# High weight tiles first, alternating lead products, and new address pads in the MLPs of a two-layer trunk

## The chip, the cores and the metric

The kernel runs on one core of one Trainium2 chip. The metric is the device time of one execution in microseconds (us); less is better. The profile is one execution on the same kind of core, taken by the hardware profiler.

## The reference

Two layers on a residual stream of 512 tokens by 1024 features, float32. The first layer mixes with multi-head latent attention, the second with gated linear attention; each is followed by an MLP with a squared ReLU. The change concerns the two MLPs (and the norm ahead of each), which hold most of the arithmetic.

```python
D_MODEL = 1024; SEQ = 512; D_FF = 4 * D_MODEL

def sq_relu_mlp(xn, w_up, w_down):
    hid = jnp.square(jax.nn.relu(xn @ w_up))
    return hid @ w_down

for i in range(DEPTH):                      # DEPTH = 2
    xn = rms_norm(x, norm_mix[i])
    mix = mla_mixer(xn, ...) if i == 0 else gla_mixer(xn, ...)
    x = x + mix.astype(x.dtype)
    x = x + sq_relu_mlp(rms_norm(x, norm_mlp[i]), mlp_w_up[i], mlp_w_down[i])
return rms_norm(x, final_norm)
```

## The kernel before

**Float32 products from three matmuls.** TensorE (PE) works on a rounded float32 type. Each operand is therefore split into a high tile (the value rounded, made by a copy on ScalarE, ACT) and a low tile (the rest, made by a subtraction on VectorE, DVE); this is `split` (L105 to L113, ACT at L110, DVE at L113). A product takes three matmuls: high weight times high input (L118), high weight times low input (L119), low weight times high input (L120), in `mm3`. `piece` makes the high and low tiles of a weight, `wh` and `wl`, in three rotating buffers each. One split of 128 by 1024 elements is shared by the 24 matmuls of a product, each with a weight of 128 by 128 and a moving operand of 128 by 256.

**Seven products in place of eight.** The MLP's two matrix products are computed block by block with the Winograd form of Strassen's scheme. `up_block(b)` makes 512 of the 4096 hidden features, in two halves of 256; the inner dimension of 1024 is split in a leading and a trailing half, the tokens in a first and a second half. Its seven products have the names "11", "21", "22" (plain inputs x0 to x3, x4 to x7) and "T1" to "T4" (combinations of inputs, tiles T0 to T3 by feature pair, made by `QuadNorm.pair`). The weights are loaded by `unit`, the combined weights are made on DVE (L884, L899, L905, L912). The steps are s0 to s7; s0 only loads and splits the first two weights of block 0, s1 is product "11", s2 "21", s5 "T1", s6 "T2", s3 "22", s7 "T3", s4 "T4". Steps end in `finish`, which multiplies by the norm's factor `rstd` (DVE, L840) and squares (ACT, L841).

`down_block(s)` takes two up blocks back to the residual stream, again in seven products (p1 to p7) of two pieces each, with the hidden values as moving operand: tile `h`, split by `operand`. The last two up blocks go through `down` or `down_final` with ordinary products. Sums stay in the tiles `sum1`, `sum6`, `sum7` and in the residual stream's own tiles `xT`.

**The lead of an MLP.** `out_proj` ends the mixer in four steps c = 0 to 3. Each adds two column tiles to `xT`, scales them for the norm (`scaled`), squares them (`square`), and makes one of the four pairs (`pair(c)`). At c = 3 it starts the MLP (`next(after)`): only s0 runs. When the projection is done the MLP goes on: the pools `stage` and `ps` close, `down` and `down_w` open, and the lead runs the steps of `lead = [blocks[b].pop(0) for b in (0, 0, 1, 1)]`: block 0's s1, then `begin` (the norm's mean by a matmul with a constant tile, L253, then `rstd`, and four subtractions in the residual stream, L1080), block 0's s2, block 1's s1, block 1's s2. Block 1's first weights (both halves of the inner dimension) come in one load of 1024 KB into the pool `down_w` (L824). After the lead the remaining steps run block by block with `down_block` steps between them.

**Order of work.** The program names the work in the order of the source; the order in each engine's queue is then chosen by a scheduler, which may move an instruction ahead of others when it takes it to be ready sooner. `tc.keep_in_program_order(i)` holds an instruction behind everything that the source has named on its engine so far; `with tc.issue_after(i)` holds what the block names on i's engine behind i. Neither makes an engine wait for an instruction's end.

**Addresses.** Pools take addresses from the left or the right end of on-chip memory, and `pad` puts some bytes (`PADS`) into a pool so that the tiles behind it move. All weight and operand tiles are multiples of 512 bytes long, so one number, the distance of the moving operand from the weight tile modulo 512 bytes, holds for all matmuls of a group. `right` and `up` move the up operands, `stage` the pools on the left.

## Time and profile before

| what | value |
|---|---|
| median of 3 runs | 1093.47 us (1093.22 to 1094.63) |
| the profiled execution, its own time | 1092.46 us |
| span of its instructions | 1090.7 us |
| PE busy in the span | 1065.7 us (98%), 7322 matmuls |
| weight loads | 981.1 us (90%) |
| DVE busy | 892.1 us (82%) |
| ACT busy | 641.0 us (59%) |
| HBM traffic | 99 GB/s over the span |

PE is the matrix engine, PEld its weight loads, DVE and ACT the two elementwise engines, POOL the general one, SP the engine whose queue issues most loads. A row of a timeline has the start in us from the span's start, the duration, engine, line, operation, tile written and tiles read, shape and count; in brackets the idle time of the engine before it and what ended it. A row of busy time by window has the stretch, its length, and for each engine the busy time and the number of instructions, then the granted clock of PE (1.00 is full), the busy share of the DMA engines and their GB/s. Ends of matmuls are modelled: the distance between two starts is what a matmul really took.

### The profile page before, as it was taken

To read this page: it belongs to the slowest core of one execution; us is meant where nothing else is said; L and a number is where in the kernel's file an instruction comes from. 1 tells how busy PE (TensorE), PEld (TensorE's weight loads), DVE (VectorE), ACT (ScalarE), POOL (GpSimd) and SP (SyncE) were. 2 spreads that over 40 slices of the span, in tenths; PEclk is the share of its full clock that TensorE was granted. 3 is DMA by queue.
4 is the path that set the end of the run, shared out by engine and by line. 5 is a ranking of instruction groups with operands and counts; after the bars stand their busy time and mean duration, and the time that the engine had idled before them with its cause. 6 is when DMAs were issued, how large, how long until landed. Compare 5 with 4: busy or idle time off the path is not lost.

```text
span 1090.7 us, 17825 instructions
## 1 busy us (share of the span) xinstructions
PE 1065.7 (98%) x7322; PEld 981.1 (90%) x7322; DVE 892.1 (82%) x1210; ACT 641.0 (59%) x934; POOL 46.6 (4%) x78
## 2 busy tenths in 40 slices
PE   8999999899999999999999999999999999999997
PEld 6788888889999999998788888887999999999986
DVE  6789878899899899977565655678899899799865
ACT  6577655555667677654334735655565666766734
POOL 6400000000000000030000000000000000000000
PEclk9999999999999999999999999999999999999999
DMA  7312113633433422251222222125424424522312
GB/s 215 87 49 78 29 32 92 198 97 117 149 104 98 155 97 97 78 190 42 53 73 78 78 78 63 53 78 173 132 65 132 141 78 133 167 71 94 134 41 78
DMA packets 99057, 108.93 MB, mean 100 GB/s; under 512 B 8112, under 2 KB 73920, under 8 KB 98976
## 3 DMA queue, kind: packets, MB, share of 16 engines
q1 hardware_dynamic: 96960, 106.57, 31.0%
q10 hardware_dynamic: 1952, 1.21, 0.4%
q8 instruction: 57, 0.93, 0.4%
q0 software_dynamic: 64, 0.02, 0.1%
q14 instruction: 24, 0.20, 0.1%
HBM read 105.69 MB, written 2.10 MB: 99 GB/s over the span
## 4 chain that ended last, share of the span: by engine, by line
PE 87%; DVE 8%; ACT 2%; issue 1%; DMA 1%; SPq 0%; ACTq 0%; DVEq 0%
PE ps L118 27%; PE ps L120 27%; PE ps L119 26%; DVE wl L113 2%; PE ps L135 2%; PE ps L1345 2%; ACT wh L110 1%; DMA wraw_ckv<-in_mla_w_in_dram 1%; DVE raw L1000 1%; DVE raw L884 1%; DVE h L113 0%; PE ps L1382 0%; PE ps L666 0%; DVE raw L912 0%; PE ps L667 0%
## 5 line engine op out<-in xcount | busy, mean ns | idle before, releaser
L110 ACT ACTIVATE wh<-raw 128x1024 fp32r<-128x1024 f32 x210 | 221.3, 1057 | 177.4 <-PE ps L119 135.9
L113 DVE TENSOR_TENSOR wl<-raw,wh 128x1024 fp32r<-128x1024 f32 x210 | 254.4, 1218 | 25.4 <-ACT wh L110 24.9
L120 PE MATMUL ps<-h,wl 128*128 128x256 f32 x672 | 188.4, 280 | 2.6 <-DVE wl L113 2.5
L118 PE MATMUL ps<-h,wh 128*128 128x256 f32 x672 | 187.9, 280 | 0.0
L119 PE MATMUL ps<-h,wh 128*128 128x256 f32 x672 | 187.8, 280 | 0.0
L120 PEld LDWEIGHTS ps<-h,wl 128*128 128x128 f32 x672 | 126.5, 188 | 3.8 <-DVE wl L113 3.8
L118 PEld LDWEIGHTS ps<-h,wh 128*128 128x128 f32 x672 | 126.3, 188 | 0.0
L119 PEld LDWEIGHTS ps<-h,wh 128*128 128x128 f32 x672 | 126.3, 188 | 0.0
L118 PE MATMUL ps<-set,wh 128*128 128x512 f32 x232 | 91.4, 395 | 1.3 <-ACT set L243 1.3
L119 PE MATMUL ps<-set,wh 128*128 128x512 f32 x232 | 90.8, 391 | 1.0 <-DVE set L244 1.0
L120 PE MATMUL ps<-set,wl 128*128 128x512 f32 x232 | 90.6, 390 | 0.0
L110 ACT ACTIVATE wh<-wraw 128x1024 fp32r<-128x1024 f32 x41 | 43.0, 1056 | 73.9 <-PE ps L120 41.5
L118 PE MATMUL ps<-wh,set 128*128 128x512 f32 x144 | 59.7, 414 | 0.0
L841 ACT ACTIVATE q<-q 128x512 f32<-128x512 f32 x64 | 40.1, 627 | 32.0 <-DVE q L840 31.9
L113 DVE TENSOR_TENSOR wl<-wraw,wh 128x1024 fp32r<-128x1024 f32 x41 | 50.0, 1222 | 10.6 <-ACT wh L110 10.5
L113 DVE TENSOR_TENSOR h<-q,h 128x1024 fp32r<-128x1024 f32 x42 | 51.2, 1218 | 7.5 <-ACT h L110 7.5
L120 PE MATMUL ps<-wh,set 128*128 128x512 f32 x144 | 56.4, 391 | 0.0
L119 PE MATMUL ps<-wl,set 128*128 128x512 f32 x144 | 56.2, 391 | 0.0
L119 PEld LDWEIGHTS ps<-set,wh 128*128 128x128 f32 x232 | 43.6, 188 | 11.0 <-DVE set L244 2.2
L118 PEld LDWEIGHTS ps<-set,wh 128*128 128x128 f32 x232 | 43.5, 188 | 11.0 <-ACT set L243 2.0
L120 PEld LDWEIGHTS ps<-set,wl 128*128 128x128 f32 x232 | 43.6, 188 | 8.9
L110 ACT ACTIVATE h<-q 128x1024 fp32r<-128x1024 f32 x42 | 44.1, 1050 | 1.3 <-DVE q L986 1.3
(490 smaller groups left out, 3003.9 us busy)
## 6 DMA issues: line engine op xcount, KB each, us to landing
raw<-in_mlp_w_down_dram SPq DMA_DIRECT2D x38, 1024.0 KB, 5.2
raw<-in_mlp_w_up_dram SPq DMA_DIRECT2D x62, 512.0 KB, 3.8
wraw<-in_gla_w_in_dram SPq DMA_DIRECT2D x11, 1024.0 KB, 5.2
wraw<-in_mla_w_o_dram SPq DMA_DIRECT2D x8, 512.0 KB, 4.8
wraw<-in_gla_w_o_dram SPq DMA_DIRECT2D x8, 512.0 KB, 4.9
raw<-in_mlp_w_up_dram SPq DMA_DIRECT2D x2, 1024.0 KB, 7.7
xT<-in_x_dram SPq DMA_DIRECT2D x6, 256.0 KB, 7.6
wraw_qn<-in_mla_w_uq_dram SPq DMA_DIRECT2D x6, 256.0 KB, 3.4
```

Of the source, the lines that this page charges most:

```text
L110: order(ACT.activation(hi, src, AF.Copy))
L113: lo_eng.tensor_tensor(lo, src, f(hi), ALU.subtract)
L118: PE.matmul(psum, wh, xh, start=start, stop=False, **kw)
L119: PE.matmul(psum, wh, xl, start=False, stop=False, **kw)
L120: PE.matmul(psum, wl, xh, start=False, stop=stop, **kw)
L135: PE.transpose(psum, src, ident[: src.shape[0], : src.shape[0]])
L841: ACT.activation(qs, qs, AF.Square)
L884: DVE.tensor_tensor(s, v["a21"], v["a22"], ALU.add)
L1000: DVE.tensor_tensor(v["S"], v["12"], v["S"], ALU.subtract)
L1345: PE.matmul(p[:, t * 64 : (t + 1) * 64].rearrange("p (n c) -> p n c", c=m), k[:, sl], later, start=True, stop=True)
```

## The change

Five things are done. In the diff, `raised` collects the ACT copies that `split` issues and `cut_at` the DVE subtractions of `piece`; `made` holds the tiles that a block finds made already.

- Inside `matmuls`, which up and down products share, all matmuls with high weight tiles are issued first, for each weight with the high and the low input, and then all with low weight tiles. An up product's two output halves are now both inside one call. The first matmul of each call is held behind everything that the source has named on PE before it.
- The lead runs block 0's s1, block 1's s1, the mean's matmul, then block 0's s2 and block 1's s2. Block 1's first weights come in two loads of 512 KB (`ahead`), with the block's other up loads queued behind them, and its high and low tiles are made ahead of block 0's s1.
- The fourth pair is no longer made in `out_proj` but in the lead, in two parts, `combine` (into a buffer of tag `q` of the pool `down`) and `combined` (its split); `combine` is queued behind the low tile of block 1's "11", the low tile of block 1's "21" behind the combination, the pair's split behind that.
- The four subtractions in the residual stream move behind block 0's last split.
- Pads: `hidden` puts 416 bytes ahead of `h` in the first MLP's `down` pool; `up` goes from 448 to 320 bytes in the second MLP; `down_w` gets 224 bytes in the second MLP.

```diff
-    PADS = dict(stage=224, right=64, up=448, masks=256, keep=128)
+    PADS = dict(stage=224, right=64, up=(448, 320), masks=256, keep=128, hidden=(416, 0), down_w=(0, 224))
...
+    raised, cut_at = [], []
...
+        def mean(self):
+            self.ms = bank("c")
+            return PE.matmul(self.ms, self.inv, self.acc, start=True, stop=True)
...
         def pair(self, k):
             pool = pool_of("up")
+            self.combined(k, self.combine(k, pool.tile([P, 4, TH], F32, tag="raw", bufs=5, name=uname("raw"))))
+
+        def combine(self, k, t):
...
+            return t
+
+        def combined(self, k, t):
...
+            i = split(t, hi, lo)
...
+            return i
...
-            nxt.pair(c)
+            if c < 3:
+                nxt.pair(c)
...
         def matmuls(p, w, k0, ks, ms, x, begin, end):
-            for k in ks:
-                for m in ms:
-                    mm3(
-                        p[:, m * TH : (m + 1) * TH],
-                        cut(w, slice(None), k - k0, slice(m * P, (m + 1) * P)),
-                        x[k],
-                        begin and k == 0 and m % 2 == 0,
-                        end and k == 3,
-                        skip_group_check=True,
-                    )
+            def one(i, j, k, m, start, stop):
...
+            steps = [(k, m) for k in ks for m in ms]
+            for k, m in steps:
+                i = one(0, 0, k, m, begin and k == 0 and m % 2 == 0, False)
+                if (k, m) == steps[0]:
+                    tc.keep_in_program_order(i)
+                one(0, 1, k, m, False, False)
+            for k, m in steps:
+                one(1, 0, k, m, False, end and k == 3)
...
             def unit(half, trail):
                 if b == 1 and half == 0:
-                    if not trail:
-                        c0 = b * FB
-                        t = wide_raw().rearrange("p a (b n) -> p (a b) n", b=2)
-                        SP.dma_start(t, w_up[:, c0 : c0 + 256].rearrange("(k p) n -> p k n", p=P))
-                        v["a12"] = t[:, KH:]
-                    return t[:, :KH]
+                    return ahead[trail]
                 t = up.tile([P, KH, 256], F32, tag="raw", bufs=5, name=uname("raw"))
                 c0 = b * FB + half * 256
-                SP.dma_start(t, w_up[trail * 512 : trail * 512 + 512, c0 : c0 + 256].rearrange("(k p) n -> p k n", p=P))
+                with tc.issue_after(made["load"].ins) if "load" in made else nullcontext():
+                    SP.dma_start(t, w_up[trail * 512 : trail * 512 + 512, c0 : c0 + 256].rearrange("(k p) n -> p k n", p=P))
                 return t
 
             def product(p, a, name, begin):
                 w = v.pop(name) if name in v else piece(a, KH, 256)
-                for j in range(2):
-                    matmuls(p, w, 0, range(KH), [j], quad[name], begin, True)
+                matmuls(p, w, 0, range(KH), range(2), quad[name], begin, True)
...
         def down_block(s):
             last = s == NB // 2 - 2
+            if s == 0:
+                pad(dp, PADS["hidden"][layer])
...
-        def begin():
-            nrm.finish()
-            for k in range(KH):
-                DVE.tensor_tensor(xT[k][:, second], xT[k][:, second], xT[k + KH][:, second], ALU.subtract)
...
-        opened("down_w")
+        pad(opened("down_w"), PADS["down_w"][layer])
...
-        lead = [blocks[b].pop(0) for b in (0, 0, 1, 1)]
-        for i, step in enumerate(lead):
-            step()
-            if i == 0:
-                begin()
+        t = wide_raw().rearrange("p a (b n) -> p (a b) n", b=2)
+        ahead = t[:, :KH], t[:, KH:]
+        for i, a in enumerate(ahead):
+            made["load"] = SP.dma_start(a, w_up[i * 512 : i * 512 + 512, FB : FB + 256].rearrange("(k p) n -> p k n", p=P))
+        kept = tc.keep_in_program_order
+        made[1]["11"] = piece(ahead[0], KH, 256)
+        with tc.issue_after(raised[-1].ins):
+            blocks[0].pop(0)()
+        blocks[1].pop(0)()
+        with tc.issue_after(cut_at[-1].ins):
+            t = nrm.combine(KH - 1, dp.tile([P, 4, TH], F32, tag="q", bufs=6, name=uname("q")))
+        kept(nrm.mean())
+        made[1]["21"] = piece(ahead[1], KH, 256)
+        kept(cut_at[-1])
+        kept(nrm.combined(KH - 1, t))
+        pad(up, PADS["up"][layer])
+        nrm.finish()
+        for b in range(2):
+            blocks[b].pop(0)()
         downs = []
         for b in range(NB):
...
+            if b == 0:
+                with tc.issue_after(cut_at[-1].ins):
+                    for k in range(KH):
+                        DVE.tensor_tensor(xT[k][:, second], xT[k][:, second], xT[k + KH][:, second], ALU.subtract)
```

## The prediction, made before the result was known

> **What bounds the kernel now.** I read the profile page first, then busy time by window over the two MLPs, then the timelines of PE, ACT, DVE and SP where PE waited.

> ```profile
> span 1090.7 us, 17825 instructions
> PE 1065.7 (98%) x7322; PEld 981.1 (90%) x7322; DVE 892.1 (82%) x1210; ACT 641.0 (59%) x934; POOL 46.6 (4%) x78
> PE 87%; DVE 8%; ACT 2%; issue 1%; DMA 1%; SPq 0%; ACTq 0%; DVEq 0%
> L110 ACT ACTIVATE wh<-raw 128x1024 fp32r<-128x1024 f32 x210 | 221.3, 1057 | 177.4 <-PE ps L119 135.9
> ```

> The chain that ended last is PE for 87% of the span, so a change gains where PE waits or where a matmul takes longer than it must. The 8% that is DVE lies mostly in the MLPs, which the change touches:

> ```profile
> core 0: us, PE busy (x) PEld busy (x) DVE busy (x) ACT busy (x) POOL busy (x), PEclk, DMA share, GB/s
> 191.20:475.70 284.50, 277.48 (x2356) 274.92 (x2355) 265.71 (x249) 184.48 (x213) 5.58 (x8) 0.99 0.38 121
> 750.20:1036.60 286.40, 278.78 (x2357) 275.96 (x2356) 265.65 (x248) 185.49 (x214) 0.00 (x0) 0.99 0.38 122
> ```

> The first window is the first MLP from its first product to its last quarter-product, the second the same of the second MLP. Of 284.5 us DVE is busy 265.7: a second engine is only 19 us behind PE, and no gain of PE can outrun it. Each window holds 1344 matmuls of up products (56 products of 24) and 1008 of down products.

> Now the lead, the first products of the first MLP, on PE:

> ```profile
> 193.95 0.28 PE L120 MATMUL ps<-x3h,wl 128*128 128x256 f32 x1
> 199.03 0.38 PE L118 MATMUL ps<-x0h,wh 128*128 128x256 f32 x1 [0.93 <-ACT wh L110]
> 199.25 0.28 PE L119 MATMUL ps<-x0l,wh 128*128 128x256 f32 x1
> 201.28 0.58 PE L120 MATMUL ps<-x0h,wl 128*128 128x256 f32 x1 [1.76 <-DVE wl L113]
> 201.66 0.42 PE L118 MATMUL ps<-x1h,wh 128*128 128x256 f32 x1
> 204.22 0.28 PE L118 MATMUL ps<-x1h,wh 128*128 128x256 f32 x1
> 206.19 0.38 PE L118 MATMUL ps<-x4h,wh 128*128 128x256 f32 x1 [0.51 <-ACT mt L867]
> 226.98 0.39 PE L118 MATMUL ps<-x4h,wh 128*128 128x256 f32 x1 [1.08 <-ACT mt L888]
> 758.02 0.39 PE L118 MATMUL ps<-x0h,wh 128*128 128x256 f32 x1 [0.93 <-ACT wh L110]
> 760.28 0.38 PE L120 MATMUL ps<-x0h,wl 128*128 128x256 f32 x1 [1.75 <-DVE wl L113]
> ```

> A matmul is drawn 0.28 us long but the next normally starts 0.11 to 0.12 later, and the one behind a stall again takes 0.1 too long, so a stall costs its bracket plus 0.28. The second block's first product waits 1.21 for its high weight tile, then, after two matmuls, 2.04 for the low one; the next start is 0.38 later instead of 0.12, 0.26 more than normal, of which 0.1 is counted. From 201.66 to 204.22 lie twelve starts, 0.213 us each: PE ran at half clock after these waits, 1.15 us lost. With 0.79 at 206.19 the lead's stalls cost 1.21 + 2.04 + 0.16 + 1.15 + 0.79 = 5.35 us. The second MLP repeats them (758.02, 760.28).

> **The lead (part one).** Before, the products run b0-11, b0-21, b1-11, b1-21 ("b0-11": first block, half 0, operand 11), and b1's weights are the late ones:

> ```profile
> 188.44 0.39 SPq L824 DMA_DIRECT2D raw<-in_mlp_w_up_dram  x1
> 197.93 2.93 ACT L110 ACTIVATE wh<-raw 128x1024 fp32r<-128x1024 f32 x3
> raw<-in_mlp_w_up_dram SPq DMA_DIRECT2D x2, 1024.0 KB, 7.7
> 201.75 1.22 DVE L113 TENSOR_TENSOR wl<-raw,wh 128x1024 fp32r<-128x1024 f32 x1
> ```

> Their load is issued at 188.44, lands 7.7 later at 196, is raised by ACT from 197.9 and cut by DVE up to about 202.9, after everything that DVE does for the norm, for x7 and for the fourth pair. After, two loads of half the size are queued ahead of the block's other loads. Their buffer no longer shares bytes with the stage pool: by the tile sizes, the first wide tile begins 224 bytes below the end of the stage pool's last tile; 416 bytes of pad in the first MLP and 224 in the second take it clear, so the load need not wait for that tile. The transfer moves from 191 to 206, where the DMA engines are 0.73 busy (row below), to before 191, where they are 0.23 (row of 176 to 191 under the rivals). SP then holds back only b0's two loads of half 1, which the T1 product needs some 12 us later. The high tile's buffer comes free with the last matmul of the output projection (190.8, b0-11 starting at 191.2), so ACT raises b1-11 by 192.1 and DVE, right after its addition at 191.2, cuts it by 193.3. PE runs b0-11 to 194.0, b1-11 to 196.7, the mean's matmul (0.95 as before, 193.95 to 194.90), b0-21 to 200.4, b1-21 to 203.1. DVE in the meantime has x7's low part and square (0.66, 0.6), the pair's four combinations (0.4 each), b1-21's cut and T3's (1.14 each start to start): 6.1 us from 193.3, done by 199.5, before b1-21 starts. Queued behind those cuts are the three steps of rstd and T1's sum and cut, some 5 us to 204.5, and with low tiles late in a product T1 can start at 203.1 on its high tile. The mean waits for acc only if the scheduler puts the combinations ahead of it, 1.6 us. So the 5.35 us go; what is late next is DVE:

> ```profile
> 191.00:206.00 15.00, 11.99 (x79) 10.77 (x77) 14.59 (x20) 8.02 (x11) 0.00 (x0) 0.89 0.73 250
> 206.00:221.00 15.00, 14.81 (x128) 14.65 (x129) 12.43 (x12) 7.48 (x10) 0.00 (x0) 1.00 0.48 141
> 221.00:236.00 15.00, 13.79 (x114) 13.19 (x113) 13.16 (x15) 9.96 (x13) 0.00 (x0) 1.00 0.45 142
> 236.00:244.00 8.00, 7.18 (x63) 7.18 (x64) 8.00 (x9) 4.59 (x7) 0.00 (x0) 1.00 0.00 0
> ```

> In 53 us DVE is busy 48.2, idle 4.8. Its work there stays: the four subtractions of L1080 (0.42 each) move from before the lead's end to behind the first block's last cut, which puts about 1.2 us more into this stretch, and T1's sum (1.2), whose raw weights can now land before 191, may move out into DVE's idle time there. So I count 4.8 per MLP, 9.6 in all, between 0 (DVE takes all back) and 10.8. The stall at 226.98 waits for an ACT copy and is left.

> **High tiles first (part two).** A product issued high, high, low per weight; now all 16 high matmuls, then the 8 low. No instruction is added, and a loss I exclude: each matmul keeps its operands, and down products switch between PSUM regions every three matmuls already. The low tile is wanted by the 17th matmul instead of the 3rd, 14 x 0.113 = 1.6 us later, and a high buffer is free after the 16th instead of the 23rd, 0.8 us sooner, for which ACT's L110 idles 135.9 us in all (page row above). The pin on each call's first matmul forbids PE to begin a product ahead of its turn, as it did before 206.19, where two matmuls of T1 stood ahead of b1-21; behind that pin waits all of PE. I cost it at nothing, since the products' weights are made in the same order on ACT and DVE; should one be late out of turn, PE waits as at 226.98, 1.3 us a time. The stalls on low tiles behind the leads:

> ```profile
> 356.60 0.38 PE L120 MATMUL ps<-T0h,wl 128*128 128x256 f32 x1 [0.81 <-DVE wl L113]
> 404.48 0.39 PE L120 MATMUL ps<-h,wl 128*128 128x256 f32 x1 [0.34 <-DVE wl L113]
> 450.42 0.39 PE L120 MATMUL ps<-h,wl 128*128 128x256 f32 x1 [0.62 <-DVE wl L113]
> 917.27 0.38 PE L120 MATMUL ps<-T0h,wl 128*128 128x256 f32 x1 [0.93 <-DVE wl L113]
> 1011.33 0.38 PE L120 MATMUL ps<-h,wl 128*128 128x256 f32 x1 [1.54 <-DVE wl L113]
> ```

> With 0.28 each they cost 1.09 + 0.62 + 0.90 + 1.21 + 1.82 = 5.64. All but a fraction of the last fit into 1.6 us. But DVE is late there because it is behind, and a PE that does not wait meets the next late tile sooner. I take two thirds, 3.8; the ends are 0 and 5.6.

> **The addresses (part three).** Pads cost no instruction. They move the moving operand against the weight tiles. From the allocation: weight tiles lie at 416 modulo 512 bytes, up operands at 480 (64 beyond), the down operand h at 192 (288 beyond). After, h in the first MLP and up operands in the second stand 192 beyond; the first MLP's up stays at 64, the second's down at 288. What the trace shows of distances:

> ```profile
> 244.86 0.28 PE L118 MATMUL ps<-h,wh 128*128 128x256 f32 x1
> 250.47 0.28 PE L118 MATMUL ps<-x4h,wh 128*128 128x256 f32 x1
> 255.92 0.28 PE L118 MATMUL ps<-h,wh 128*128 128x256 f32 x1
> 407.16 0.28 PE L118 MATMUL ps<-x4h,wh 128*128 128x256 f32 x1
> 412.82 0.28 PE L118 MATMUL ps<-h,wh 128*128 128x256 f32 x1
> 619.67 0.28 PE L118 MATMUL ps<-set,ADh 128*128 128x256 f32 x1
> 621.47 0.28 PE L118 MATMUL ps<-set,ADh 128*128 128x256 f32 x1
> ```

> Forty-eight down matmuls at 288 take 244.86 to 250.47, 117 ns each; forty-eight up at 64 take 113.5; the same at 407.16 takes 117.9; fifteen at distance 0 (619.67 to 621.47) 120. So 64 has two beats, kept from one stall to the next. In the second MLP it ran about half and half: the window's 286.4 less 12.5 of stalls, 0.8 of the mean and 1008 x 117, over 1344, is 115.6. Distance 192 is nowhere in the trace. Its ends are 113.3 and 120; 288 is nearest (96 bytes, 64 is 128 away), so I take 117.0: down unchanged, up 1344 x 1.4 = +1.9 us. By the ends: down -3.7 to +3.0, up -3.1 to +5.9.

> [...]

> **Sum.** -9.6 - 3.8 + 1.9 = -11.5 on the profiled execution's 1092.46 (span 1090.7), 1081.0. The median of the runs, 1093.47, is 1.0 above it: 1082.0.

> **Rivals.** (a) Distance 192 keeps the fast beat, 113.3 throughout: -13.4 - 6.8, 1073.3. For it: 64 does so for long stretches; against: nothing shows it for 192. (b) Addresses do nothing at 192, the beats following stalls alone: -13.4, 1080.1. [...] (c) DVE is the bound of the lead and gives all of part one back: -3.8 + 1.9, 1091.6. For it the 14.59 of 15.00; against it the 2.6 and 1.8 us of DVE idle right after. (d) Slower: 192 is worse than every distance of narrow matmuls in the trace.

> ```profile
> 176.00:191.00 15.00, 15.00 (x67) 12.40 (x67) 12.28 (x18) 7.53 (x12) 0.00 (x0) 1.00 0.23 66
> 1074.12 0.39 PE L120 MATMUL ps<-set,hl 128*128 128x512 f32 x1
> 1076.21 0.40 PE L120 MATMUL ps<-set,hl 128*128 128x512 f32 x1
> ```

> Wide matmuls at distance 0 take 227 ns (15.00 over 66 intervals), and in the last stage, at 224, only 32 from 192, 232 (nine in 2.09 us), 2.3% more. On 120 that is 122.8: 1008 x 5.8 + 1344 x 7.2 = +15.5, with -13.4 a loss of 2.1: 1095.6. It decides from 121.9 ns on, where the offsets eat the 13.4.

> **How the numbers follow.** Forecast 0.47, a 0.22, b 0.13, c 0.10, d 0.08. Time 1082.0; its own range is 1077 to 1088. The range 1073 to 1090 takes in a and b and leaves out c and d, 0.18. Some 0.2% (2.2 us) is what a measurement of this kernel can tell from no change: faster 0.47 + 0.22 + 0.13 + 0.03 of c = 0.85, same 0.07, slower 0.08.

> **What would show it.** Right: no PE stall on wh or wl between the first and the ninth up product of either MLP, granted clock 1.00 there, the fifth product starting near 203 instead of 209 after a first at 191; no bracket "DVE wl" over 0.3 us later; DVE above 95% in the MLP windows. The beat of first-MLP h and second-MLP up rows gives the third term alone: 24 starts in 2.72 us is rival a, over 2.92 rival d. Wrong: PE waiting on rstd or acc in the lead, on T3's low part, or at a pinned first matmul.

## The result, and the profile after

The changed kernel takes 1087.49 us (median of 4 runs, 1087.19 to 1089.39) against 1093.57 of the kernel before on the same chip: ratio 0.9944, 95% interval 0.9931 to 0.9956. The profiled execution took 1087.19, 5.3 below that of before; the prediction said 11.5 below. The medians differ by 6.1. The sign was right and the size about half. One execution of all those reported here, one of e7, took 1506.32 us at a granted clock of 0.654 and is left out of every median and ratio.

The page of the changed kernel. PE holds 88% of the chain instead of 87, DVE its 8%; ACT's idle time for PE in L112 (before: L110) went from 135.9 us to 95.2:

```profile
span 1085.5 us, 17842 instructions
PE 1063.5 (98%) x7322; PEld 981.6 (90%) x7322; DVE 890.9 (82%) x1210; ACT 641.2 (59%) x934; POOL 45.1 (4%) x78
PE 88%; DVE 8%; issue 1%; DMA 1%; ACT 1%; SPq 0%; DVEq 0%; ACTq 0%
L112 ACT ACTIVATE wh<-raw 128x1024 fp32r<-128x1024 f32 x210 | 221.2, 1057 | 158.1 <-PE ps L814 95.2
```

Where PE waits, in the answers on waits of the kernel before and then of the one after (engine and line that wait, releaser: us in all, times, longest):

```profile
PE ps L120 <- DVE wl L113: 7.8, 7, 1.8
PE ps L118 <- ACT wh L110: 3.5, 4, 0.9
PE ps L118 <- ACT mt L888: 2.1, 2, 1.1
```

```profile
PE ps L814 <- DVE q L933: 5.5, 4, 2.2
PE ps L814 <- ACT wh L112: 3.9, 3, 1.6
PE ps L814 <- DVE wl L115: 2.0, 2, 1.4
```

The waits on low tiles fall from 7.8 to 2.0 us, as meant. A wait stands there that the kernel before did not have: L933, DVE's read of the bank into which T3 was summed and into which T4, next on PE, goes on summing. The lines shown add up to 13.4 and 11.4 us: the new wait takes 5.5 of the 7.9 us that the low tiles and the copies of L888 gave back.

The lead itself went as predicted in the first MLP, up to the fifth product (203.14; forecast near 203, before 209). Then (timeline of PE after):

```profile
190.97 0.28 PE L814 MATMUL ps<-x0h,wh 128*128 128x256 f32 x1
203.14 0.28 PE L814 MATMUL ps<-T0h,wh 128*128 128x256 f32 x1
216.84 0.38 PE L814 MATMUL ps<-T0h,wh 128*128 128x256 f32 x1 [2.23 <-DVE q L933]
217.77 0.37 PE L814 MATMUL ps<-T1l,wh 128*128 128x256 f32 x1
221.30 0.29 PE L814 MATMUL ps<-T0h,wh 128*128 128x256 f32 x1
233.80 0.39 PE L814 MATMUL ps<-T0h,wh 128*128 128x256 f32 x1 [1.03 <-DVE q L933]
242.39 2.04 PE L814 MATMUL ps<-h,wh 128*128 128x256 f32 x16
```

From 217.77 to 221.30 PE runs at half clock, as it did before at 201.66 (busy time by window of after; the clock is the third number from the end):

```profile
218.00:221.00 3.00, 3.00 (x16) 3.00 (x16) 2.79 (x3) 2.64 (x3) 0.00 (x0) 0.50 0.00 0
```

So wait and half clock moved from 199 to 217. The first down product starts 51.42 us after the first product, before 53.62: 2.2 us of the expected 4.8. What DVE does ahead of L933 (its timeline after):

```profile
211.29 1.42 DVE L1142 TENSOR_TENSOR xT<-xT 128x256 f32<-128x256 f32 x4
212.64 1.22 DVE L930 TENSOR_TENSOR raw<-raw,raw 128x1024 f32<-128x1024 f32 x1
213.77 0.68 DVE L926 TENSOR_TENSOR q<-ps,mt 128x512 f32<-128x512 f32 x1
214.37 1.21 DVE L115 TENSOR_TENSOR wl<-raw,wh 128x1024 fp32r<-128x1024 f32 x1
215.51 0.68 DVE L858 SCALAR_TENSOR_TENSOR q<-q,rstd 128x512 f32<-128x512 f32 x1
216.11 0.68 DVE L933 TENSOR_TENSOR q<-ps,mt 128x512 f32<-128x512 f32 x1
```

No gap anywhere: DVE is behind, and the four subtractions that the change put there (L1142) stand in the same queue. In the second MLP a further wait remains. ACT takes x7h, its square and the pair's scaling (749.39 to 752.05, with 0.90 us of idle time between) ahead of the raise of b1-11 (its high tile), and PE waits 1.45 us:

```profile
751.95 1.04 ACT L112 ACTIVATE wh<-raw 128x1024 fp32r<-128x1024 f32 x1
753.05 0.38 PE L814 MATMUL ps<-x0h,wh 128*128 128x256 f32 x1 [1.45 <-ACT wh L112]
```

The MLPs as wholes, by windows as before (the same stretches, first up matmul to last quarter-product), are 1.2 and 4.1 us shorter:

```profile
core 0: us, PE busy (x) PEld busy (x) DVE busy (x) ACT busy (x) POOL busy (x), PEclk, DMA share, GB/s
190.97:474.25 283.28, 280.02 (x2357) 279.13 (x2356) 264.76 (x252) 186.09 (x215) 5.50 (x8) 0.99 0.34 109
748.70:1031.05 282.35, 274.26 (x2357) 272.25 (x2356) 266.03 (x252) 186.22 (x216) 0.00 (x0) 1.00 0.36 118
```

Two sums from the matmul records split this. "Stalls": over all intervals from start to start above 135 ns, the excess over 115 ns (the mean's matmul left out). "Beat": the mean of the other intervals, some 1320 of up products (distance of moving operand beyond the weights in brackets) and 1005 of down products (h).

| kernel | first MLP: stalls us; up ns; h ns | second MLP: stalls; up; h |
|---|---|---|
| before | 11.40; 114.78 (64); 117.12 (288) | 12.51; 115.56 (64); 116.84 (288) |
| after | 5.79; 117.84 (64); 117.71 (192) | 10.66; 114.21 (192); 116.71 (288) |

The stalls fell by 7.5 us, of which the beat took 4.0 back in the first MLP's up products, whose own distance was not changed, and 0.6 in h; the second MLP's up products gave 1.8 and its h 0.1. That is 4.8 of the 5.3.

### The profile page after: what moved, and what is told of

The parts are those of the page before. It is cut to its first block, busy times and chain, and to the rows that moved or that the text cites. A ratio compares the mean times of both kernels' runs of the same rounds, so it can differ in the third digit from the quotient of the medians.

```text
span 1085.5 us, 17842 instructions
## 1 busy us (share of the span) xinstructions
PE 1063.5 (98%) x7322; PEld 981.6 (90%) x7322; DVE 890.9 (82%) x1210; ACT 641.2 (59%) x934; POOL 45.1 (4%) x78
## 3 DMA queue, kind: packets, MB, share of 16 engines
q10 hardware_dynamic: 1952, 1.21, 0.4%
## 4 chain that ended last, share of the span: by engine, by line
PE 88%; DVE 8%; issue 1%; DMA 1%; ACT 1%; SPq 0%; DVEq 0%; ACTq 0%
PE ps L814 42%; PE ps L120 13%; PE ps L122 12%; PE ps L121 12%; DVE wl L115 3%; PE ps L137 2%; PE ps L1378 2%; DMA wraw_ckv<-in_mla_w_in_dram 1%; ACT wh L112 1%; DVE q L858 0%; PE ps L1415 0%; PE ps L680 0%; PE ps L681 0%; PE ps L679 0%; DVE h L115 0%
## 5 line engine op out<-in xcount | busy, mean ns | idle before, releaser
L112 ACT ACTIVATE wh<-raw 128x1024 fp32r<-128x1024 f32 x210 | 221.2, 1057 | 158.1 <-PE ps L814 95.2
L814 PE MATMUL ps<-h,wh 128*128 128x256 f32 x1344 | 171.2, 280 | 0.0
L814 PEld LDWEIGHTS ps<-h,wh 128*128 128x128 f32 x1344 | 163.5, 188 | 0.0
L814 PE MATMUL ps<-h,wl 128*128 128x256 f32 x672 | 92.5, 280 | 1.4 <-DVE wl L115 1.4
L120 PE MATMUL ps<-set,wh 128*128 128x512 f32 x232 | 91.4, 394 | 1.0 <-ACT set L245 1.0
L112 ACT ACTIVATE wh<-wraw 128x1024 fp32r<-128x1024 f32 x41 | 43.0, 1056 | 74.4 <-PE ps L122 41.5
L814 PEld LDWEIGHTS ps<-h,wl 128*128 128x128 f32 x672 | 84.9, 189 | 1.6 <-DVE wl L115 1.6
L120 PE MATMUL ps<-wh,set 128*128 128x512 f32 x144 | 59.7, 414 | 0.0
L120 PEld LDWEIGHTS ps<-set,wh 128*128 128x128 f32 x232 | 43.5, 188 | 10.5 <-ACT set L245 1.7
L112 ACT ACTIVATE h<-q 128x1024 fp32r<-128x1024 f32 x42 | 44.1, 1051 | 3.8 <-DVE q L1006 1.5
L814 PE MATMUL ps<-T0h,wh 128*128 128x256 f32 x128 | 33.4, 284 | 7.9 <-DVE q L933 5.5
L120 PE MATMUL ps<-hh,wh 128*128 128x512 f32 x96 | 37.4, 389 | 0.0
## 6 DMA issues: line engine op xcount, KB each, us to landing
raw<-in_mlp_w_down_dram SPq DMA_DIRECT2D x38, 1024.0 KB, 5.2
wraw<-in_gla_w_in_dram SPq DMA_DIRECT2D x11, 1024.0 KB, 5.2
wraw<-in_mla_w_in_dram SPq DMA_DIRECT2D x1, 1024.0 KB, 9.0
```

The costliest lines, as they stand in the source:

```text
L112: raised.append(order(ACT.activation(hi, src, AF.Copy)))
L120: PE.matmul(psum, wh, xh, start=start, stop=False, **kw)
L814: return PE.matmul(p[:, m * TH : (m + 1) * TH], w[i][:, k - k0, m * P : (m + 1) * P], x[k][j], start=start, stop=stop, skip_group_check=True,)
```

## The experiments

Four at a time shared one chip and one set of runs of the kernel before (medians 1094.19, 1095.11 and 1093.64), so ratios are compared across sets. Theories at the start: (L) the new lead is worth some 5 us per MLP; (D) DVE takes it back; (O) the order alone removes the waits on low tiles; (H) h at 192 puts the up products beside it into the slow beat; against H, that the new lead's entry does, or that addresses do nothing. Old lead and new lead are compared four times: e1 with e3, e4 with e2, and below e11 with e5 and e10 with e9.

**One part at a time.** e1 is the changed kernel with the old distances, e2 the kernel before with the new ones, e3 the kernel before with the order and pin alone (the pin holds a call's first matmul behind all that the source named on PE before it), e4 the changed kernel without the order.

```
e1: PADS up=(448, 448), hidden=(0, 0), down_w=(416, 224)      # in the changed kernel
e2: PADS up=(448, 320), hidden=(416, 0), down_w=(0, 224)      # in the kernel before
e3: matmuls() and product() of the changed kernel             # in the kernel before
e4: for j in range(2): matmuls(p, w, 0, range(KH), [j], ...)  # triples per weight again, pin kept
```

> The changed kernel with the old address distances in both MLPs (up operands 64 beyond the weights, h 288). In the changed kernel's trace the first MLP's up products, at 64 as before, take 117.8 ns a matmul (before 114.8), h at 192 117.7 (before 117.1), and the second MLP's up products at 192 take 114.2 (before 115.6 at 64). Theory 'h holds the beat' (down products at 192 between the up products keep these in the slow beat): the first MLP returns to 114.8 and 117.1, -4.6, the second loses 1.9: 1087.5 - 2.7 = 1084.8. Theory 'entry phase' (the new lead starts the slow beat and nothing ends it, whatever the distances): the first MLP keeps 117.8, h gains 0.6, the second loses 1.9: 1088.8. [...]

> The kernel before with the new address distances alone: order and lead as before. 'h holds the beat': the first MLP's up products go from 114.8 to 117.8 ns (+4.0) and h from 117.1 to 117.7 (+0.6), the second MLP's up products gain 1.9: 1093.5 + 2.7 = 1096.2. 'Entry phase': only h +0.6 and the second MLP's -1.9: 1092.2. 'Addresses do nothing': 1093.5. My prediction's term for it was +1.9: 1095.4.

> The kernel before with the high tiles' matmuls first in each product and the pin, lead and distances as before. My prediction's term: -3.8 (two thirds of 5.64 us of later stalls on low tiles), 1089.7, with the lead's waits on wl shortened at most by 2 x 1.6 us more, 1086.5. If the order alone puts up products into the slow beat (3.1 ns x 1344 = 4.1 us per MLP) they give all of it back: 1093 to 1098. The trace tells which: no brackets 'DVE wl' over 0.3 us behind the leads in either case, up products at 114 to 116 ns or at 117.8.

> The changed kernel with the old order high, high, low per weight in every product; lead and distances as changed. If the order is worth the 3.8 of my prediction: 1087.5 + 3.8 = 1091.3, with stalls on wl back in the lead and behind it. If the lead has left the low tiles no longer late: 1087.5. If the new order is what holds the first MLP in the slow beat, its up products return to 114.8 ns (-4.0) and the total is 1087.5 + 3.8 - 4.6 = 1086.7, with the stalls on wl back all the same.

| run | us | ratio, interval | first MLP: stalls; up; h | second MLP |
|---|---|---|---|---|
| e1 lead + order | 1086.80 | 0.9922 (0.9904 to 0.9939) | 7.79; 114.39 (64); 116.89 (288) | 9.70; 115.06 (64); 117.15 (288) |
| e2 distances | 1091.43 | 0.9970 (0.9955 to 0.9985) | 7.59; 117.37 (64); 116.64 (192) | 14.79; 113.73 (192); 116.76 (288) |
| e3 order | 1085.62 | 0.9914 (0.9895 to 0.9933) | 7.62; 114.63 (64); 117.20 (288) | 8.23; 115.16 (64); 117.30 (288) |
| e4 lead + distances | 1095.22 | 1.0007 (0.9994 to 1.0020) | 9.02; 117.26 (64); 115.41 (192) | 15.78; 114.35 (192); 116.75 (288) |

The order alone gives 8.6 us, more than the whole change. The lead adds nothing to it (e1 against e3: 1.2 us slower, intervals overlapping). Of these 1.2 the MLPs hold little: from first up matmul to last quarter-product they take 0.1 us more in e1, and its first MLP starts 1.9 us later (193.41 against 191.54). Without the order lead and distances together give nothing (e4), and against the distances alone (e2) the lead makes it 3.8 us slower, outside both intervals. In e3 the stalls ahead of the first down product fall from 8.73 and 8.55 us to 6.25 and 6.14, those behind from 2.67 and 3.96 to 1.37 and 2.09. The leads of e3 by window (first product to first down product), to be set beside 53.62 and 54.16 of before:

```profile
191.54:243.44 51.90, 47.40 (x389) 45.74 (x388) 49.46 (x54) 31.26 (x40) 0.00 (x0) 1.00 0.47 152
746.66:798.52 51.86, 47.62 (x389) 45.82 (x388) 49.46 (x54) 31.14 (x40) 0.00 (x0) 1.00 0.47 152
```

The granted clock is 1.00: here, where the wait on the low tile no longer stands right behind that on the high tile, the half clock does not come. The first low matmul starts 0.38 us after the matmul before it (at 201.19), where it was 2.03 us in the kernel before:

```profile
199.32 0.38 PE L799 MATMUL ps<-x0h,wh 128*128 128x256 f32 x1 [0.93 <-ACT wh L110]
201.58 0.50 PE L799 MATMUL ps<-x0h,wl 128*128 128x256 f32 x2
```

The wait at T4 is there with the old lead too, and in e4 with the old order (9.2 us on L933), so it is not the new lead's alone. At the same distances and order the new lead adds waits on ACT's raises (answers on waits of e3, where the read is L922, then of e1):

```profile
PE ps L799 <- DVE q L922: 5.1, 4, 1.6
PE ps L799 <- ACT wh L110: 1.9, 2, 0.9
```

```profile
PE ps L814 <- ACT wh L112: 6.5, 6, 1.6
PE ps L814 <- DVE q L933: 3.9, 4, 1.2
```

H holds for the beat: the first MLP's up products return to 114.4 in e1 and go to 117.4 in e2, old lead and old order. The time did not follow in e2, whose first MLP has 3.8 us of stalls less; that a slower PE meets fewer late tiles fits this, and the 2.3 us of stalls more in its faster second MLP, but was not tested by itself. The 1091.4 fits the 1092.2 of the entry theory better, though its trace refutes that theory.

**Distances and DVE's load.** e5 is e3 with up at 192 in both MLPs, e6 has h at 192 there too. e7 and e8 are the changed kernel with the four subtractions taken off DVE, or put off by one block.

```
e5: PADS up=320, for both MLPs                   # e3 otherwise
e6: PADS up=320, hidden=416, for both            # e3 otherwise
e7: POOL.tensor_tensor(xT[k][:, second], ...)    # was DVE
e8: if b == 1: with tc.issue_after(cut_at[-1].ins): ...   # was b == 0
```

> The kernel before with the high-first order and the pin, lead as before, and up operands 192 beyond the weights in both MLPs (h stays at 288). From the runs so far: with h at 288, up at 64 took 114.4 to 115.6 ns, at 192 113.7 to 114.4. If the distance sets it, the order-alone kernel (114.63 and 115.16 in its two MLPs, 1085.6) gains about 0.9 ns x 2688 = 2.4 us: 1083.2. If up at 192 beside h at 288 makes no difference to 64: 1085.6.

> As the last one, with h at 192 too in both MLPs, so that both kinds of products stand at one distance. If what keeps up products slow is that h stands at 192 (117.3 to 117.8 in the three kernels that have it): 3 ns x 2688 = 8 us more than the kernel with h at 288, 1091. If it is the mixture of two distances (64 and 192) that does it, up products stay at 113.7 to 114.4 and h goes from 116.8 to between 113.3 and 116.6: 1083.2 less up to 2016 x 3.5 = 7 us, 1076 to 1083.

> The changed kernel with the four subtractions of each MLP, which stand ahead of the copy that PE waits for, on GpSimd. If DVE's work bounds the lead: 1.4 us of DVE less in each MLP, stalls of the lead 5.8 and 7.9 fall by about 1.4 each, 1087.5 - 2.8 = 1084.7. If the stalls are only an order of PE that cannot give way (pin) or ACT's late raises: 1087.5. GpSimd takes 0.81 us for such a 128x256 addition elsewhere in the trace (four: 3.3 us, hidden), if it does not slow DVE down beside it.

> The changed kernel with the same four subtractions still on DVE, but behind the second block's last cut, some 20 us later. If only their place ahead of that copy costs: -1.4 in each MLP, 1084.7, the stall of 2.5 us in the first MLP falls to 1.1. If DVE's whole work over the first 50 us bounds: the stall of 2.5 shrinks and a later one grows by as much, 1087.5.

| run | us | ratio, interval | first MLP: stalls; up; h | second MLP |
|---|---|---|---|---|
| e5 | 1082.63 | 0.9888 (0.9873 to 0.9903) | 8.10; 114.06 (192); 116.73 (288) | 8.91; 114.38 (192); 116.73 (288) |
| e6 | 1087.36 | 0.9933 (0.9911 to 0.9956) | 9.25; 116.99 (192); 117.78 (192) | 9.72; 115.44 (192); 115.66 (192) |
| e7 | 1088.74 | 0.9940 (0.9917 to 0.9964) | 8.05; 117.78 (64); 114.02 (192) | 11.11; 114.33 (192); 116.73 (288) |
| e8 | 1089.81 | 0.9948 (0.9930 to 0.9965) | 6.19; 117.83 (64); 117.71 (192) | 12.49; 114.30 (192); 116.77 (288) |

e5 came out as expected and beats both kernels. In 100 us of the first MLP without a stall PE starts 851 matmuls after, 870 in e5; in e6 851, and in its second MLP 884 (windows of after, e5, e6 and e6, ahead of each the stretch):

```profile
250.00:350.00 100.00, 100.00 (x851) 100.00 (x850) 95.14 (x85) 61.61 (x70) 0.00 (x0) 1.00 0.37 119
```

```profile
250.00:350.00 100.00, 100.00 (x870) 100.00 (x870) 96.43 (x87) 63.05 (x72) 0.00 (x0) 1.00 0.38 121
```

```profile
250.00:350.00 100.00, 100.00 (x851) 100.00 (x850) 95.18 (x85) 63.59 (x71) 0.00 (x0) 1.00 0.39 126
800.00:900.00 100.00, 100.00 (x884) 100.00 (x884) 96.14 (x86) 62.33 (x71) 0.00 (x0) 1.00 0.35 111
```

So with everything at 192 one stretch holds 117.5 ns a matmul and another 113.1: neither theory on e6 holds as it was put. Its seven runs spread from 1084.1 to 1092.0, those of e5 from 1082.2 to 1083.9. In the three tables with beats here, up products beside h at 288 took 113.7 to 115.6 ns (13 MLPs), beside h at 192 115.4 to 117.8 (7 MLPs).

e7 and e8 brought nothing; their times are nearest the second expectation of each. In e8 the first MLP's stall at block 0's T4 shrinks from 2.51 to 2.25 us from start to start and that at block 1's grows from 1.31 to 1.96, as a bound by DVE's whole work would have it; in e7, with that work 1.4 us less, PE waits longer. With the subtractions gone from that place L933 starts 26.0 us after the first product in e7, 25.1 in the changed kernel (DVE's timeline in e7, then PE's):

```profile
214.59 1.22 DVE L930 TENSOR_TENSOR raw<-raw,raw 128x1024 f32<-128x1024 f32 x1
215.73 0.68 DVE L926 TENSOR_TENSOR q<-ps,mt 128x512 f32<-128x512 f32 x1
216.33 1.22 DVE L115 TENSOR_TENSOR wl<-raw,wh 128x1024 fp32r<-128x1024 f32 x1
217.46 0.68 DVE L858 SCALAR_TENSOR_TENSOR q<-q,rstd 128x512 f32<-128x512 f32 x1
218.06 1.22 DVE L917 TENSOR_TENSOR raw<-raw,raw 128x1024 f32<-128x1024 f32 x1
219.20 0.68 DVE L933 TENSOR_TENSOR q<-ps,mt 128x512 f32<-128x512 f32 x1
```

```profile
219.94 0.39 PE L814 MATMUL ps<-T0h,wh 128*128 128x256 f32 x1 [3.10 <-DVE q L933]
```

The scheduler put L917, the next block sum, into the freed place, ahead of L933 (after: behind it, at 216.71); in e8 it did the same. So neither run shows what L933 would do without work put in its way: L917 takes 1.14 us of the queue from start to start where the four subtractions took 1.35.

**T4's wait, the lead at the better distances, the pin.** e9 is e5 with block 0's T4 product behind block 1's T1, and block 1's behind block 2's first; e10 is the same displacement and the same distances with the new lead; e11 the changed kernel with up at 192 and h at 288 in both MLPs; e12 is e5 without the pin.

```
e9, e10: blocks[1].insert(1, blocks[0].pop()); blocks[2].insert(1, blocks[1].pop())
         i -= b == 2                             # the down steps of block 2 stay where they were
e11:     PADS up=(320, 320), hidden=(0, 0), down_w=(416, 224)
e12:     no tc.keep_in_program_order on a product's first matmul
```

> Order high first, old lead, up at 192 and h at 288 in both MLPs (1082.6), and block 0's T4 product behind block 1's T1 product, block 1's behind block 2's first product, so that another product lies between T3 and the T4 that adds to the bank that DVE reads out after T3. If the stalls there (1.4 and 1.8 us in each MLP, 6.5 in all) come from T3 and T4 standing next to each other: 5 to 6.5 less, 1076 to 1077.5, and no wait of PE on that read. If DVE's work over the first 50 us bounds the lead: the waits move to other products' low tiles or banks, 1082.6, and the first down product starts 51.6 us after the first product as before.

> As the last one, with the new lead of the changed kernel. If the new lead's gain of 4.8 us per MLP was there and was lost in the waits at T4 (four of them, 1.0 to 2.5 us each in the changed kernel): 1082.6 - 6 - up to 9.6 = 1067 to 1077, and below the kernel with the old lead. If DVE bounds the lead: the same as the old lead with T4 displaced, within 2 us.

> The changed kernel (new lead, order high first) with up at 192 and h at 288 in both MLPs. The old lead at these distances took 1082.6. If the lead is worth nothing, as order alone (1085.6) beside lead and order at the old distances (1086.8) says: 1082.6 to 1084. My prediction's term for the lead: -9.6, 1073. Against the changed kernel (first MLP's up products 117.8 ns) the distances give 3.7 ns x 1344 = 5 us less: 1082.5.

> Order high first, old lead, up at 192 and h at 288 (1082.6), without the pin on each product's first matmul, so that another product may fill the wait at T4. If the pin costs these waits (6.5 us in all): 1076 to 1079. If the order's gain of 8.6 came from the pin, because the scheduler else puts matmuls of late products first: back towards 1087 to 1091. If the pin does nothing: 1082.6.

| run | us | ratio, interval | stalls ahead of the first down product, first and second MLP | first product to first down product |
|---|---|---|---|---|
| e5 (above) | 1082.63 | 0.9888 (0.9873 to 0.9903) | 6.76, 6.56 | 51.59, 51.59 |
| e9 | 1084.81 | 0.9917 (0.9899 to 0.9936) | 9.59, 6.31 | 54.01, 51.31 |
| e10 | 1087.46 | 0.9955 (0.9932 to 0.9977) | 8.69, 10.94 | 53.18, 55.45 |
| e11 | 1084.18 | 0.9913 (0.9898 to 0.9928) | 6.54, 7.95 | 51.79, 52.68 |
| e12 | 1082.26 | 0.9896 (0.9879 to 0.9913) | 6.47, 6.79 | 51.13, 51.09 |

The waits at T4 do not go, they change their name (e9's answer on waits; L880 is the ACT copy that seeds the next bank):

```profile
PE ps L799 <- ACT ps L880: 6.3, 2, 3.5
PE ps L799 <- DVE wl L113: 2.8, 5, 1.1
```

e11 is the changed kernel with the better distances: 0.9913 against 0.9944, so the distances as changed cost some 3 us against these. Beside e5 it shows once more that the new lead gives nothing (1.6 us slower by the medians, intervals overlapping, but each of its four runs above each of e5's); e10 is 2.7 us slower than e9. With the old lead the pin neither costs nor gives. The leads of e11 and of e12 by window:

```profile
191.48:243.27 51.79, 46.99 (x388) 45.53 (x387) 48.95 (x56) 31.39 (x41) 0.00 (x0) 1.00 0.36 120
746.03:798.71 52.68, 46.53 (x388) 45.08 (x387) 48.96 (x56) 31.40 (x41) 0.00 (x0) 1.00 0.36 117
```

```profile
191.38:242.51 51.13, 46.74 (x388) 44.87 (x387) 48.75 (x53) 30.78 (x40) 0.00 (x0) 1.00 0.49 155
745.25:796.34 51.09, 46.37 (x389) 44.51 (x387) 48.71 (x53) 30.75 (x40) 0.00 (x0) 1.00 0.47 154
```

In the changed kernel and all twelve others the leads last 51.1 to 55.5 us, with DVE busy for 47.9 to 50.1 of them. Whatever was moved, PE waited at least 5.7 us there. That the new lead's gain does not stay is shown, and that PE then waits for tiles and reads made late by DVE and ACT. That DVE's load is the cause is argued: in the changed kernel its read L933 is the largest of these waits, in e1 and e11 ACT's raises are (6.5 and 6.8 us, of which two of some 0.8 in each follow a DVE sum). Whether the amount of work or the order of the queues decides is open; e7, with 1.4 us of DVE's work less and another order, speaks against the amount alone. A kernel with L933 put first in DVE's queue was not run.

## Why the prediction was half right, by its steps

- **The lead, -9.6: this step failed.** It read the 5.35 us of waits rightly, and the four products did run as drawn (203.14). It failed at "what is late next is DVE": it found DVE 48.2 of 53 us busy and still booked 4.8 of the 5.35 as gain, on the 4.8 us of DVE's idle time. Measured by the medians: +1.2 (e1 against e3), +1.6 (e11 against e5), +2.7 (e10 against e9) and +3.8 (e4 against e2), the first no different from 0, the last a loss clear of noise; from first up matmul to last quarter-product of both MLPs +0.1, +1.2, +2.3 and +1.5. DVE's idle time was taken for room that the moved work would fill, and it did not. Rival c had the amount right for this term, and DVE as its cause in part. The parts of DVE's work listed for the lead (x7's, the pair's, two cuts) add up to 5.1 us, not 6.1; in the trace they last to 199.85, with one more cut between, and nothing hung on it.
- **High tiles first, -3.8: mis-sized, -8.6 in e3** (interval 7.3 to 11.5 by the ratio). The mechanism was right: the low-tile waits go. But the low-tile wait inside the lead, 2.04 us, with the 1.15 of half clock behind it, was booked to the lead alone, though 16 high matmuls instead of 2 ahead of the first low one cover it. By stalls e3 gains 4.9 us in the leads and 3.2 behind them; the prediction's count for those behind, 3.8, was nearly right. The two errors cancel in part, which is why the sum looks better than its terms: that the measured time lies inside the range given is partly luck.
- **The pin at nothing: right** (e12). The prediction named a wait at a pinned first matmul as what would make it wrong. T4's is one, but without the pin PE waits as long in the lead (6.47 and 6.79 us against 6.76 and 6.56).
- **The addresses, +1.9: near in size, wrong in place.** By beats the change cost 2.7 (4.0 + 0.6 - 1.8 - 0.1). The second MLP's up products at 192 are faster (114.21), not at 117.0, and nearer the 113.3 that rival a had for them; in e5, where only the pad of up differs from e3, 2.9 us are gained by the ratios. The cost came from the first MLP's up products, which the prediction left as they were because their distance stays at 64. Its assumption that a product's beat hangs on its own distance alone is what fell. Nor is the sign the same everywhere: with the old lead and order the same distances gave 2.8 us by the medians (e2). Rival b (addresses do nothing) falls too: in the first MLP e2, which differs from the kernel before in its pads alone, shows 117.4 for 114.8, and with the new order 64 and 192 gave 114.6 (e3) and 114.1 (e5).
- **The signs to look for.** No wait on wh or wl in the first nine products: true in the first MLP, not in the second (1.45 us on ACT). Clock 1.00 there: 0.5 from 218 to 221. No later bracket on wl over 0.3: none in the first MLP, 0.53 and one of 1.4 in the second. DVE above 95% in the MLPs: 93.5 (264.76 of 283.28) and 94.2.

## What to carry to other kernels

When a second engine is busy for nine tenths of a stretch, a wait taken away from the first engine there can come back a few microseconds later under another name, as in the four comparisons here. The second engine's idle time is an upper bound for such an edit and no estimate of it (here 4.8 us per MLP were booked and none came): look at the order of its queue behind the edit, and try the edit without the others first. Reordering work so that the late operand is wanted later is worth more than it looks where two waits in a row are followed by half clock, as in the kernel before (199.03 and 201.28, 1.15 us more). When operands are moved in memory, time every product of the loop, also those that were not moved (the first MLP's up products stayed at 64 and went from 114.8 to 117.4 ns in e2).

The best versions here are e5 and e12, the order with up at 192 and h at 288 and the old lead: 1082.6 and 1082.3 us, some 11 to 12 below the kernel before and some 5 to 6 below the changed one.
